# A third raw weight buffer in the gates' own pool, and the weight sums' work buffer from the trunk on

## The chip, the cores and the metric

The kernel runs on one core of a Trainium2 chip. The metric is device time in microseconds (us) from the start to the end of one execution. Its engines are TensorE (PE, with PEld for its weight loads), VectorE (DVE), ScalarE (ACT), GpSimd (POOL) and SyncE (SP). SP computes nothing here: it issues most of the DMAs, one after the other in the order of its queue, and a DMA that has to wait holds those behind it in the queue. POOL issues some DMAs as well.

## The reference

One layer of a streaming encoder for two groups of tokens that share the weights: 1024 prompt frames and 32 sample frames, width 1024, all in f32.

```python
z = rms_norm(x, g_mix) @ w_in
q, k, v, ch, cb, cc, ga, gb = split(z)
a  = window_attention(q, k, v, sink) @ w_attn_out
bo = (cb * causal_conv3(cc * ch)) @ w_conv_out
x  = x + (sigmoid(ga) * a + sigmoid(gb) * bo) @ w_mix_out
x  = x + memory_attention(rms_norm(x, g_cross) @ w_cq, mem_k, mem_v) @ w_co
x  = x + square(relu(rms_norm(x, g_mlp) @ w_up)) @ w_down
y  = rms_norm(x, g_final)
```

The keys and values of the window, the convolution's state and the memory's keys and values are returned beside y.

## The kernel before, in words

The 1056 tokens lie on the free axis in three chunks (384, 384, 288) and the features on the 128 partitions. A weight is a tile of 128 x 1024 f32 (512 KB). For f32 accuracy every operand is split in two: `split` casts the raw tile to `wh` (ACT, L129) and subtracts that to get `wl` (DVE, L130), and a product is three matmuls (`gemm`, L193 to L195; `product` for half a weight, L864 to L866).

Weights come in the order of the list `worder`. `fetch_w` (L147) issues the load of the next raw tile on SP (L155) and puts it on the list `fetched`; `issue_w` takes the first of that list, or fetches if there is none, and splits it into `wh` and `wl` (three buffers each); `next_w` keeps three split weights ready. Raw tiles have two buffers, tag `wr`. From the gates on there is a third: when the dictionary `third` is not empty, it counts the fetches, and every third one takes the tile `ws` of the pool `W["pool"]`, which has one buffer.

That tile is also the work buffer of the weight sums. The gates, and parts of the MLP, use products of a Strassen kind, which need sums of weight quarters. `sum_step` makes them piece by piece on POOL: it issues the load of a piece (L712, L714) into one of two tiles (`ws` and `xacc`, in turn), adds four times in the tile loaded by the step before (L719), and issues that tile's store (L723, L725) to `gsum_d` (gates), `wsum_d` (w_down) or `usum_d` (w_up). There are 50 pieces: 14 for the gates, 32 for w_down, 4 for w_up, in this order. The steps are called among the other work from the fourth attention host to the end of the attention output; in the order of the program all are done before the gates. The trace gives the two tiles the names `ws` and `xacc` by their buffers.

The stages around the change are, in the order of the program:
- the hosts: 32 weights of w_in (convolution inputs marked C, H and B, queries, keys), with window attention between their chunks; `do_KS` loads the key cache `ck` of a group of heads (L518, one buffer);
- the attention output: eight weights for three chunks (`do_attn_out`), with the last sum steps between;
- the gates: seven pairs, `gate_pair(f)` for f = 1 to 7. A pair uses four weights, w1 = w_in 34+f, w4 and w3 (the two sums of pair f), and w2 = w_in 42+f. It loads the attention's output (`load_a`, L928), stores the gated one (`attended`, L920), and `pump` loads and splits operands (L794, L795, L799). It begins, for f = 1, with `third["n"] = 2` and a fetch: that of w3, which so takes the third buffer;
- the trunk: conv_out, mix and the memory attention for each chunk, and then the MLP (up, down), where the sums of w_up and w_down are read.

The order in each engine's queue is made before the run by the framework's planner. It runs through a plan of its own, with its own estimates of durations, and puts an instruction in its engine's queue when, in the plan, its inputs and its buffer are there. The order of the program decides between instructions that are ready together. `pin` (`keep_in_program_order`) puts an instruction behind the one traced before it on its engine; the sum steps are pinned on POOL, the loads of weights on SP are not. Pools with `reuse_waits="tile"` may be opened on memory of closed pools: a new tile waits for the old tiles that lay there.

Memory: the pool `gtop` of the gates (`Y["top"]`) holds, per partition, eight tiles N4 and one each of s1, u2 and v, of 1536 bytes, 16,896 in all. It is opened where `ytop` (16 x 1152 = 18,432 bytes, operands of the attention output's third chunk) was.

```python
        if third and third["n"] % 3 == 0:
            raw = W["pool"].tile([P, 4, 256], F32, tag="ws", name=nm("wr3")).rearrange("p q c -> p (q c)")
        else:
            raw = wp.tile([P, 1024], F32, tag="wr", bufs=2, name=nm("wr"))
        src = weight(worder[wpos[0] + len(fetched)])
        sp.dma_start(raw.rearrange("p (i c) -> p i c", i=4) if len(src.shape) == 3 else raw, src)
```

Of the kernel before, what the change touches and what calls it, by code (L numbers as in the profile page):

```python
# [10 lines left out]
F32 = mybir.dt.float32  # L11
# [7 lines left out]
P = 128  # L19
# [4 lines left out]
NF = 8  # L24
# [16 lines left out]
def hybrid_step(ctx: ExitStack, tc: tile.TileContext, io):  # L41
# [5 lines left out]
    def nm(s):  # L47
        uid[0] += 1
        return f"{s}_{uid[0]}"

    def opened(name, **kw):
        cm = tc.tile_pool(name=name, **kw)
        return cm, cm.__enter__()

    def closed(cm):
        cm.__exit__(None, None, None)
# [43 lines left out]
    def acc_tile(shape):  # L100
        return ps.tile(shape, F32, tag="acc", bufs=n_acc, name=nm("acc"))
# [3 lines left out]
    def tmp(n, dt=F32):  # L105
        return tp.tile([P, n], dt, tag="ct", bufs=NCT, name=nm("ct"))
# [25 lines left out]
    def weight(key):  # L132
        name, *at = key
        if name in ("w_down", "w_sum"):
            q, j, t = at
            return (wsum_d if name == "w_sum" else io[name])[j, t, :, :, q].rearrange("i p c -> p i c")
        if name == "g_sum":
            return gsum_d[at[0]][:, at[1]].rearrange("p h c -> p (h c)")
        src = io[name]
        for j in at:  # L140
            src = src[j]
        return src

    fetched = []
    third = {}

    def fetch_w():  # L147
        if third:
            third["n"] += 1
        if third and third["n"] % 3 == 0:  # L150
            raw = W["pool"].tile([P, 4, 256], F32, tag="ws", name=nm("wr3")).rearrange("p q c -> p (q c)")
        else:
            raw = wp.tile([P, 1024], F32, tag="wr", bufs=2, name=nm("wr"))
        src = weight(worder[wpos[0] + len(fetched)])
        sp.dma_start(raw.rearrange("p (i c) -> p i c", i=4) if len(src.shape) == 3 else raw, src)  # L155
        fetched.append(raw)

    def issue_w():
        if not fetched:
            fetch_w()  # L160
        raw = fetched.pop(0)
        key = worder[wpos[0]]
        hi = wp.tile([P, 1024], F32R, tag="wh", name=nm("wh"))
        lo = wp.tile([P, 1024], F32R, tag="wl", name=nm("wl"))
        if kept.get(key) is not None:
            sp.dma_start(lo.bitcast(F32), kept[key])
            act.copy(hi, raw)
        else:
            split(hi, lo, raw)
            if key in kept:  # L170
                kept[key] = dram.tile([P, 1024], F32, name=nm("wl_d"))
                sp.dma_start(kept[key], lo.bitcast(F32))
        ready.append((worder[wpos[0]], (hi, lo)))
        wpos[0] += 1
# [39 lines left out]
    def xacc_tile():  # L214
        xacc[0] = tp.tile([P, 1056], F32, tag="xacc", name=nm("xacc"))
        return xacc[0]
# [59 lines left out]
    W = {}  # L276
# [11 lines left out]
    def norm_x():  # L288
# [7 lines left out]
        def load_x():  # L296
            for c, (o, n) in enumerate(CH):
                raw = raw_tile()[:, : NF * n].rearrange("p (f t) -> p f t", f=NF)
                for h in range(4):
                    sp.dma_start(raw[:, 2 * h : 2 * h + 2], io[f"x{c}"][:, 2 * h : 2 * h + 2])  # L300
                    if c == h == 0:
                        sp.dma_start(prm, io["params"])
                        fetch_w()
                if c == 0:
                    fetch_w()
                    fetch_w()
                raws.append(raw)
# [345 lines left out]
    def gate_slot(c, f):  # L653
        n = CH[c][1]
        return slot(ga_pool, f"Ga{c}", n, F32) if f < 3 else slot(G["pool"], f"Gb{c}", n, F32)
# [36 lines left out]
    pieces = [("g", f, q) for f in PAIRS for q in range(2)]  # L692
# [42 lines left out]
    for i, h in enumerate(hosts):  # L735
        kv, p = i // 8, i % 8
# [26 lines left out]
    Y = {}  # L763
# [27 lines left out]
    def pump(n):  # L791
        for into, at, t, get in coming:
            hi, lo = into[at] = (get(), get())
            pin(act.copy(hi, t))  # L794
            pin(dve.tensor_sub(lo, t, hi.bitcast(F32)))  # L795
        coming.clear()
        for into, at, src, cols, get in wanted[:n]:
            t = cols() if callable(cols) else tmp(cols)
            sp.dma_start(t, src)  # L799
            coming.append((into, at, t, get))  # L800
        del wanted[:n]
# [57 lines left out]
    def product(acc, w, half, acts, start):  # L859

        wh, wl = w
        for k, (hi, lo) in enumerate(acts):
            a = slice(512 * half + k * P, 512 * half + k * P + P)
            pe.matmul(acc, wh[:, a], hi, start=(start and k == 0), stop=False, skip_group_check=True)  # L864
            pe.matmul(acc, wh[:, a], lo, start=False, stop=False, skip_group_check=True)  # L865
            pe.matmul(acc, wl[:, a], hi, start=False, stop=(k == 3), skip_group_check=True)  # L866
# [22 lines left out]
    def gate_c2(w):  # L889
        n = CH[2][1]  # L890
        a = ps.tile([P, n], F32, tag="pt", bufs=2, name=nm("pa"))
        gemm(a, w, xg[2])
        return a
# [14 lines left out]
    def gate_pair(f):  # L908
        def take(key):
            k, w = ready.pop(0)  # L910
            assert k == key, (k, key)
            return w

        def into(t, x):
            act.activation(t, x, AF.Sigmoid)
            return t

        def attended(c, t):
            dve.tensor_mul(t, t, la[c])
            sp.dma_start(m1_d[c][:, f], t)  # L920

        la = {}

        def load_a(c):
            if (c, f) in sa:
                return
            la[c] = tmp(CH[c][1])
            sp.dma_start(la[c], a_d[c][:, f])  # L928

        op = lambda kind: [gop[kind, k] for k in range(4)]  # L930
        w1 = take(("w_in", 34 + f))
        if f == 1:
            assert not pieces and "new" not in W
            third["n"] = 2
            fetch_w()
        load_a(0)
        load_a(2)
        A, B, C = (acc_tile([P, 384]) for _ in range(3))
        product(A, w1, 0, op("b11"), True)
        s1 = Y["top"].tile([P, 384], F32, tag="s1", name=nm("s1"))  # L940
        act.copy(s1, A)
        issue_w()
        if f < NF - 1:
            fetch_w()
        product(A, w1, 1, op("b21"), False)
        attended(0, into(tmp(384), A))
        pump(4 if f == 1 else 1)
        if (2, f) not in sa:
            a2 = gate_c2(w1)
            t = tmp(CH[2][1])  # L950
            dve.tensor_mul(t, a2, R[2])
            attended(2, into(t, t))
        issue_w()
        fetch_w()
        w4 = take(("g_sum", f - 1, 0))
        product(B, w4, 0, op("t2"), True)
        load_a(1)
        u2 = Y["top"].tile([P, 384], F32, tag="u2", name=nm("u2"))
        dve.tensor_sub(u2, B, s1)
        sum_step()  # L960
        pump(4 if f == 1 else 1)
        w3 = take(("g_sum", f - 1, 1))
        product(C, w3, 1, op("n1"), True)
        v = Y["top"].tile([P, 384], F32, tag="v", name=nm("v"))
        dve.tensor_add(v, C, s1)
        product(B, w3, 0, op("n3"), False)
        g22 = gate_slot(1, f)
        dve.tensor_sub(g22, B, v)
        sg[1][f] = into(g22, g22)
        pump(0)  # L970
        sum_step()
        product(C, w4, 1, op("b22"), False)
        t = tmp(384)
        dve.tensor_sub(t, C, u2)
        attended(1, into(t, t))
        issue_w()
        fetch_w()
        w2 = take(("w_in", 42 + f))
        product(B, w2, 1, op("n4"), False)
        g21 = gate_slot(0, f)  # L980
        dve.tensor_sub(g21, B, s1)
        sg[0][f] = into(g21, g21)
        sum_step()
        issue_w()
        fetch_w()
        a2 = gate_c2(w2)
        g2 = gate_slot(2, f)
        dve.tensor_mul(g2, a2, R[2])
        sg[2][f] = into(g2, g2)
# [18 lines left out]
    for f in PAIRS:  # L1008
        worder.extend([("w_in", 34 + f), ("g_sum", f - 1, 0), ("g_sum", f - 1, 1), ("w_in", 42 + f)])
        item(lambda f=f: gate_pair(f))  # L1010
# [6 lines left out]
    def after_gates():  # L1017
        nonlocal m_cm, mpool, cr_cm, cr
        assert not pieces and "new" not in W
        closed(x_cm)  # L1020
        xacc_tile()
        m_cm, mpool = opened("mpool", bufs=18, reuse_waits="tile")
        cr_cm, cr = opened("cross", bufs=1, reuse_waits="tile", side="right")

    item(after_gates)


# [243 lines left out]
    top = {}  # L1271
# [711 lines left out]
```

## Time and profile before

| | us |
|---|---|
| median of 3 runs | 1853.06 (1849.84 to 1855.01) |
| the profiled execution | 1852.53 |
| its span | 1850.8 |
| PE busy | 1727.6 (93%) |
| DVE busy | 1180.8 (64%) |
| ACT busy | 853.8 (46%) |
| POOL busy | 567.9 (31%) |
| mean DMA rate | 189 GB/s |

The mean granted clock of TensorE is 0.971 of full speed. In the profile's page the span is cut in 40 equal slices; a digit is the busy share of a slice in tenths. A row of waits names who waited, for whom, the total in us, how often, and the longest. A row of a timeline gives start and duration in us, engine, line, operation, what is written and from what, how many instructions are merged, and in brackets the idle time before and what ended it. A row of windows gives a stretch, its length, then each engine's busy time with its instructions, the clock, the DMA share and GB/s. A row of DMA issues gives what is loaded or stored, the queue, how many, the size, and the median time in us from issue to landing. A row of groups gives line, operation and shapes, count, busy time, the mean of one in ns, and the idle time before.

### The profile page before, as it was taken

Reading aid. Unit: us, or ns where it says so; the run is one execution under the profiler, and the core shown is the slowest. Engines: PE = TensorE matmul, PEld = TensorE weight load, DVE = VectorE, ACT = ScalarE, POOL = GpSimd, SP = SyncE. Lnnn points to the kernel's source line nnn. Section 1 sums busy time; section 2 is a strip of 40 time slices with the busy share of each in tenths; the row PEclk is TensorE's granted clock in tenths of the full one; section 3 lists DMA queues with packets and bytes.
Section 4 is the critical chain, followed back from the end, with each engine's and each line's share of the span. In section 5 each row is a group of like instructions: output and inputs, shape, how many; then the busy total and the mean of one; then the engine's idle time right before and its main releaser. Section 6 shows DMA issues by size and latency. Waiting matters only on the chain.

```text
span 1850.8 us, 32562 instructions
## 1 busy us (share of the span) xinstructions
PE 1727.6 (93%) x12250; PEld 1713.2 (93%) x12250; DVE 1180.8 (64%) x2270; ACT 853.8 (46%) x1660; POOL 567.9 (31%) x651
## 2 busy tenths in 40 slices
PE   8999999999999940699999999999999999999998
PEld 8999999999999940699999998999999999999998
DVE  7776767767667610444656777868766677546575
ACT  8644535344344210333445565566444454333353
POOL 0026464643544445200122513001555620100121
PEclk9999999999999975799999999999999999999999
DMA  5323343434348863454876566765766686555554
GB/s 181 116 95 135 109 144 128 158 128 139 134 152 306 284 221 125 140 184 139 270 262 207 195 215 226 254 223 199 238 227 223 220 288 229 181 191 168 191 173 162
DMA packets 182221, 349.75 MB, mean 189 GB/s; under 512 B 19744, under 2 KB 102976, under 8 KB 181936
## 3 DMA queue, kind: packets, MB, share of 16 engines
q1 hardware_dynamic: 167008, 295.07, 47.1%
q0 software_dynamic: 15056, 52.60, 7.9%
q8 instruction: 96, 1.57, 0.3%
q14 instruction: 61, 0.50, 0.1%
HBM read 252.82 MB, written 94.19 MB: 187 GB/s over the span
## 4 chain that ended last, share of the span: by engine, by line
PE 81%; DMA 8%; POOL 5%; DVE 2%; issue 2%; ACT 1%; SPq 0%; DVEq 0%; ACTq 0%; POOLq 0%
PE acc L193 10%; PE acc L195 10%; PE acc L194 10%; PE acc L1768 6%; PE acc L1770 6%; PE acc L1769 6%; PE acc L864 6%; PE acc L866 6%; PE acc L865 6%; DMA wsum_d<-xacc 2%; DMA wsum_d<-ws 2%; POOL ws L719 2%; POOL xacc L719 2%; PE pc L865 2%; PE pc L866 2%
## 5 line engine op out<-in xcount | busy, mean ns | idle before, releaser
L129 ACT CAST wh<-wr 128x1024 fp32r<-128x1024 f32 x226 | 237.3, 1050 | 502.4 <-PE acc L1769 123.8
L130 DVE TENSOR_TENSOR wl<-wr,wh 128x1024 fp32r<-128x1024 f32 x226 | 292.2, 1293 | 200.6 <-ACT wh L129 198.9
L193 PE MATMUL acc<-X,wh 128*128 128x384 f32 (+1 forms) x864 | 282.1, 327 | 7.7 <-ACT wh L129 7.7
L194 PE MATMUL acc<-X,wh 128*128 128x384 f32 (+1 forms) x864 | 279.2, 323 | 0.0
L195 PE MATMUL acc<-X,wl 128*128 128x384 f32 (+1 forms) x864 | 278.6, 323 | 0.2 <-DVE wl L130 0.2
L269 POOL TENSOR_TENSOR xacc<-xacc,ct 128x384 f32<-128x384 f32 (+1 forms) x56 | 75.5, 1352 | 400.6 <-ACT ct L267 399.0
L193 PEld LDWEIGHTS acc<-X,wh 128*128 128x128 f32 x864 | 163.1, 189 | 8.3 <-ACT wh L129 7.7
L194 PEld LDWEIGHTS acc<-X,wh 128*128 128x128 f32 x864 | 163.4, 189 | 0.6
L195 PEld LDWEIGHTS acc<-X,wl 128*128 128x128 f32 x864 | 163.0, 189 | 0.8 <-DVE wl L130 0.8
L195 PE MATMUL acc<-Y,wl 128*128 128x384 f32 (+1 forms) x432 | 139.8, 324 | 2.1 <-DMA wl<-wl_d 2.1
L194 PE MATMUL acc<-Y,wh 128*128 128x384 f32 (+1 forms) x432 | 139.8, 324 | 0.0
L193 PE MATMUL acc<-Y,wh 128*128 128x384 f32 (+1 forms) x432 | 139.4, 325 | 0.3 <-ACT Y L774 0.3
L864 PE MATMUL acc<-X,wh 128*128 128x384 f32 x112 | 38.3, 343 | 91.4 <-ACT wh L129 91.4
L864 PEld LDWEIGHTS acc<-X,wh 128*128 128x128 f32 x112 | 21.5, 192 | 91.7 <-ACT wh L129 91.7
L1769 PE MATMUL acc<-n,wh 128*128 128x264 f32 x352 | 100.2, 285 | 0.0
L1768 PE MATMUL acc<-n,wh 128*128 128x264 f32 x352 | 100.2, 285 | 0.0
L1770 PE MATMUL acc<-n,wl 128*128 128x264 f32 x352 | 100.0, 285 | 0.0
L129 ACT CAST PTh<-pt 128x512 fp32r<-128x512 f32 (+3 forms) x94 | 45.9, 517 | 112.4 <-PE pt L582 111.7
L1049 POOL TENSOR_TENSOR ct<-ct,ct 128x384 f32<-128x384 f32 (+1 forms) x21 | 23.1, 1100 | 233.4 <-DMA wr<-in_w_conv_out 142.6
L719 POOL TENSOR_TENSOR ws<-ws 128x256 f32<-128x256 f32 x100 | 86.0, 860 | 5.6
L719 POOL TENSOR_TENSOR xacc<-xacc 128x256 f32<-128x256 f32 x100 | 83.8, 838 | 5.5 <-DMA xacc<-in_w_in 0.2
L195 PEld LDWEIGHTS acc<-Y,wl 128*128 128x128 f32 x432 | 81.6, 189 | 2.4 <-DMA wl<-wl_d 2.4
(422 smaller groups left out, 5643.4 us busy)
## 6 DMA issues: line engine op xcount, KB each, us to landing
wr<-in_w_in SPq DMA_DIRECT2D x53, 512.0 KB, 3.7
wr<-in_w_up SPq DMA_DIRECT2D x53, 512.0 KB, 4.3
wr<-wsum_d SPq DMA_DIRECT2D x40, 512.0 KB, 3.4
wr<-in_w_conv_out SPq DMA_DIRECT2D x24, 512.0 KB, 4.1
wr<-in_w_mix SPq DMA_DIRECT2D x24, 512.0 KB, 5.4
wr<-in_w_down SPq DMA_DIRECT2D x24, 512.0 KB, 3.6
wl<-wl_d SPq DMA_DIRECT2D x18, 512.0 KB, 4.8
n_d<-Z SPq DMA_DIRECT2D x32, 264.0 KB, 4.1
```

Of the source, the lines that this page charges most:

```text
L129: act.copy(hi, src)
L130: dve.tensor_sub(lo, src, hi.bitcast(F32))
L193: pe.matmul(out, wh[:, a], hi, start=(k == 0), stop=False)
L194: pe.matmul(out, wh[:, a], lo, start=False, stop=False)
L195: pe.matmul(out, wl[:, a], hi, start=False, stop=(k == len(acts) - 1))
L719: pin(pool_e.tensor_tensor(t[:, to], t[:, x], t[:, y], op=ALU.add))
L864: pe.matmul(acc, wh[:, a], hi, start=(start and k == 0), stop=False, skip_group_check=True)
L865: pe.matmul(acc, wh[:, a], lo, start=False, stop=False, skip_group_check=True)
L866: pe.matmul(acc, wl[:, a], hi, start=False, stop=(k == 3), skip_group_check=True)
L1768: pe.matmul(a, wh[:, s], hi, start=(t == 0 and k == 0), stop=False, skip_group_check=True)
L1769: pe.matmul(a, wh[:, s], lo, start=False, stop=False, skip_group_check=True)
L1770: pe.matmul(a, wl[:, s], hi, start=False, stop=(t == 1 and k == 7), skip_group_check=True)
```

## The change

The third buffer's pool becomes an entry of `third`. In the gates, from f = 1, it is a tile `ws` of the gates' own pool `gtop`, 4096 bytes more a partition. At the beginning of the last pair (f = 7) `third` is emptied, so that the fetches of that pair (its w2, conv_out 0 to 2) go to the two `wr` buffers. Behind the gates, in `after_gates`, `third` is filled again with the count at 0 and the sums' pool `W["pool"]`: the third fetch from there (conv_out 5) takes the work buffer `ws`. The assertion that all sum pieces are done at f = 1 goes; the sum steps are called where they were.

```diff
@@ fetch_w
         if third and third["n"] % 3 == 0:
-            raw = W["pool"].tile([P, 4, 256], F32, tag="ws", name=nm("wr3")).rearrange("p q c -> p (q c)")
+            raw = third["pool"].tile([P, 4, 256], F32, tag="ws", name=nm("wr3")).rearrange("p q c -> p (q c)")
         else:
@@ gate_pair
         if f == 1:
-            assert not pieces and "new" not in W
-            third["n"] = 2
+            third.update(n=2, pool=Y["top"])
             fetch_w()
+        if f == NF - 1:
+            third.clear()
@@ after_gates
         closed(x_cm)
         xacc_tile()
+        third.update(n=0, pool=W["pool"])
```

## The prediction

> **What bounds the kernel now.** I read the page's engine slices first, then the waits between 660 and 770 us, then the queues of PE, SP and POOL in order of time. TensorE is busy 93% of the span, and the share is lost in one place:
>
> ```profile
> span 1850.8 us, 32562 instructions
> PE   8999999999999940699999999999999999999998
> PEclk9999999999999975799999999999999999999999
> ```
>
> Slices 14 to 16 (46.3 us each) hold nearly all of PE's idle time. The waits there, then SP's own:
>
> ```profile
> PE acc L864 <- ACT wh L129: 91.4, 1, 91.4
> ACT wh L129 <- DMA wr<-gsum_d: 88.1, 1, 88.1
> ...
> SPq L155 <- DMA ws<-in_w_up: 73.0, 2, 72.3
> ```
>
> PE waits 91.4 us once, for a split that waits for a load that SP does not issue. The orders of PE and SP show where:
>
> ```profile
> 657.39 0.34 PE L864 MATMUL acc<-X,wh 128*128 128x384 f32 x1
> ...
> 666.55 0.33 PE L865 MATMUL acc<-X,wh 128*128 128x384 f32 x1
> 666.73 0.34 PE L866 MATMUL acc<-X,wl 128*128 128x384 f32 x1
> 758.42 0.69 PE L864 MATMUL acc<-X,wh 128*128 128x384 f32 x1 [91.36 <-ACT wh L129]
> ...
> 889.50 0.34 PE L193 MATMUL acc<-Y,wh 128*128 128x384 f32 x1
> ...
> 655.34 0.42 SPq L928 DMA_DIRECT2D ct<-a_d  x1
> ...
> 669.33 1.52 SPq L799 DMA_DIRECT2D ct<-bc_d  x3
> 753.77 7.34 SPq L155 DMA_DIRECT2D wr<-gsum_d  x3
> ```
>
> This is the first gate pair (f = 1): w1's products (from 657.39) and w4's first are done, and the product with the operand n1 needs `w3`, the sum (g_sum, 0, 1). Its raw load is the first to go to the third buffer, which today is the weight sums' work buffer `ws`. The data in DRAM were written long before; the buffer is what is late. So the stage is bound by the end of the sums, which POOL works through alone, one piece a step: load, four adds, store, and the next load waits for that store.
>
> ```profile
> 555.97 0.56 POOL L725 DMA_DIRECT2D wsum_d<-xacc  x1 [0.41 <-POOL xacc L719]
> ...
> 670.92 0.57 POOL L725 DMA_DIRECT2D wsum_d<-ws  x1 [0.41 <-POOL ws L719]
> ...
> 680.23 0.57 POOL L725 DMA_DIRECT2D wsum_d<-xacc  x1 [0.41 <-POOL xacc L719]
> ...
> 709.88 0.57 POOL L725 DMA_DIRECT2D wsum_d<-xacc  x1 [0.41 <-POOL xacc L719]
> ...
> 718.25 0.57 POOL L725 DMA_DIRECT2D wsum_d<-ws  x1 [0.41 <-POOL ws L719]
> ...
> 749.98 1.45 POOL L723 DMA_DIRECT2D usum_d<-ws  x2 [0.41 <-POOL ws L719]
> ```
>
> Beside the attention output (555.97 to 670.92, 11 steps) a step takes 10.45 us; alone (680.23 to 709.88, 4 steps) 7.41. After the 18th `wsum` store at 718.25 the four `usum` pieces take 31.7 us more, and the last lands 3.8 us after its start, at 753.77.
>
> **The change, part by part.**
>
> *The first raw load (gain 91.4 us, less 2).* The buffer moves into the gates' own pool. That pool opens on the memory of `ytop`, whose tiles are read last by the attention output's last chunk, which ends where w1's matmuls begin, at 657.4; so the load can go then at the earliest.
>
> ```profile
> wr<-gsum_d SPq DMA_DIRECT2D x1, 512.0 KB, 4.2
> ...
> wr<-in_w_in SPq DMA_DIRECT2D x3, 512.0 KB, 6.0
> ...
> L129 ACT CAST wh<-wr 128x1024 fp32r<-128x1024 f32 x226 | 237.3, 1050 | 502.4 <-PE acc L1769 123.8
> L130 DVE TENSOR_TENSOR wl<-wr,wh 128x1024 fp32r<-128x1024 f32 x226 | 292.2, 1293 | 200.6 <-ACT wh L129 198.9
> ...
> 666.20 2.98 ACT L794 CAST Y<-Gb 128x384 fp32r<-128x384 f32 x7
> ```
>
> Landing takes 4.2 to 6.0 us beside the attention output, the cast 1.05: ready at 663 to 665, before PE asks at 667.1; the wait would be 0. The other bound is a cast queued behind the activation splits that ACT runs until 669.2 (2.1 after PE asks, plus its own 1.05): 3.2. I take 2, nearer the upper bound, because SP also has loads and stores of this pair to issue then. A wait of 2 us should leave the clock alone:
>
> ```profile
> 670.00:680.00 10.00, 0.00 (x0) 0.00 (x0) 2.80 (x5) 0.00 (x0) 4.51 (x7) 0.57 0.62 221
> ```
>
> A mean of 0.57 over ten microseconds, in a page row that falls from full to 5 tenths, says that the clock fell some 1.4 us into them, 4 after PE's last matmul.
>
> *The work buffer from the trunk on (cost 23 us).* Here I differ from the change's wording. In the last pair the third buffer is dropped, and `n` starts at 0 behind the gates; the third trunk fetch (conv_out weight 5) takes `ws`. That is after the gates in program order, but not in SP's queue. The planner puts a load into the queue as soon as its buffer is free in the plan. The key cache of the second attention group shows it:
>
> ```profile
> 96.55 0.33 SPq L518 DMA_DIRECT2D ck<-in_cache_k  x1
> ...
> 192.93 0.30 ACT L129 CAST ckh<-ck 128x128 fp32r<-128x128 f32 x1
> ```
>
> That load was queued 96 us ahead of its use, right when its one buffer came free. So the trunk's `ws` load will stand in SP's queue where the plan thinks that the sums end, and SP will halt there until they really end. Both times have to be estimated.
>
> When does the plan end the sums? POOL's queue tells, in the hosts' stage:
>
> ```profile
> 387.64 0.59 POOL L725 DMA_DIRECT2D wsum_d<-xacc  x1 [0.42 <-POOL xacc L719]
> ...
> 396.06 0.57 POOL L725 DMA_DIRECT2D wsum_d<-ws  x1 [0.28 <-POOL S L559]
> 399.06 0.18 POOL L644 COPY cvt<-u 128x2 f32<-128x2 f32 x1 [2.43 <-DVE u L626]
> 399.41 0.53 POOL L714 DMA_DIRECT2D ws<-in_w_down  x1 [0.16 <-issue]
> 399.94 0.79 POOL L645 COPY cvt<-u 128x2 f32<-128x2 f32 x1
> ```
>
> L644 and L645 wait for two successive DVE products behind the same PE chunk, and the sum's next load L714, which waits for the store, was queued between them. In the plan, then, the store landed between them too: measured against PE, the plan's step there is the chip's, 396.06 - 387.64 = 8.4, less 0.2 for a copy in it, 8.2. I let it vary by 0.6. If the plan holds 8.2 through the attention output, where the chip needs 10.45, then it has the 18th store at 555.97 + 17 x 8.2 = 695.4; the `usum` pieces at 31.7 plus 3 x 0.8 (8.2 less 7.41) take it to 729.5 and a landing 0.7 longer than 3.8 to 734. With the 2 us above, SP gets there at 736, gates under way for 76 of their 138 us (657.4 to 667.1 and 758.4 to 889, less 2.5 for the slow clock; an estimate from PE's rows).
>
> When do the sums end? They now run beside the gates.
>
> ```profile
> 551.00:657.00 106.00, 105.71 (x675) 105.39 (x674) 67.43 (x94) 38.23 (x73) 48.62 (x61) 1.00 0.84 295
> ...
> 767.00:875.00 108.00, 108.00 (x670) 108.00 (x669) 54.91 (x80) 41.96 (x66) 0.00 (x0) 1.00 0.51 169
> ```
>
> Gates alone move 169 GB/s; the sums' two 512 KB a step add 100, together 269 against 295 beside the attention output. So a step is nearer 10.45 than 7.41: I take 9.8. From 670.92, six steps and 0.9 for the first `w_up` load give 730.6, the `usum` pieces 31.7 plus two longer steps of 2.4 give 767, landing 770 (bounds 754 and 777).
>
> SP is then held from 736 to 770. PE lives on what is fetched:
>
> ```profile
> 828.13 0.33 SPq L155 DMA_DIRECT2D wr<-gsum_d  x1
> ...
> 843.81 1.05 ACT L129 CAST wh<-wr 128x1024 fp32r<-128x1024 f32 x1 [0.60 <-PE acc L865]
> ```
>
> Counted by fours (four fetches, four casts a pair), this is the same weight: 15.7 us. PE stops at about 752 and starts again at 770 plus 4.65 (753.77 to 758.42 today), 774.7: idle 23.
>
> Whether the gates slow the sums rests on what a store takes:
>
> ```profile
> wsum_d<-xacc POOLq DMA_DIRECT2D x5, 512.0 KB, 5.7
> ...
> wsum_d<-xacc POOLq DMA_DIRECT2D x3, 512.0 KB, 2.9
> ```
>
> 5.7 us beside the attention output (551 to 660), 2.9 alone (680 to 720). With the shorter landing throughout, the sums would keep today's end, 754, PE would be idle for 754 + 4.65 - 752 = 6.6, and the sum would be 1771, a rival below. That is what a page of the Trainium skill, "DMA: Bandwidth & Descriptors", section "Anatomy of one DMA — SWDGE (gpsimd) path", comes to: it gives a transfer from GpSimd 2.0 us plus its bytes by 436 GB/s, an estimate of 3.2 for 512 KB, with no term for what runs beside it. The stage with traffic does not agree, 5.7.
>
> *Two buffers for six fetches (cost 1 us).* The last pair's own weight and conv_out 0 to 4 share two raw buffers. A buffer's turn is 6.0 plus 1.05 plus 1.29, 8.3, so 4.2 a weight, against 24 matmuls 0.18 apart (666.55, 666.73), 4.3. It just hides, under the weights fetched before; bounds 0, and 3 if each load waits 1 us in SP's queue (six by 0.5). I take 1.
>
> *Everything else* has one answer: the same adds, stores, casts and matmuls are issued, and the sums are read only in the MLP, at the end of the kernel.
>
> **Sum.** The profiled execution took 1852.53 (span 1850.8), 0.5 below the median of 1853.06. 91.4 - 2 - 23 - 1 = 65.4; 1852.5 - 65.4 = 1787.
>
> **The rivals.**
> - *SP never stops: the plan's sums end no earlier than the chip's* (a plan that slows its DMAs as the chip does, a step of 9.8 or more for 8.2; each 0.1 is worth 2.1 us by the 21 steps' worth above). Then 91.4 - 2 - 1: 1764. Against it the tie at 399 us; for it, that the tie comes from a stage with less traffic.
> - *The gates do not slow the sums* (a step of 7.41): 1771, as above. Against it the landings of 5.7.
> - *SP stops much sooner*: a plan step of 6.1 puts the load at 692, and PE stops at 708. Of the six steps 3.8 are done by then, 2.2 run alone (16.3), and with 0.9, 31.7 and 3.8 the sums end at 761; PE restarts at 765.7 after 57.7 idle: gain 91.4 - 2 - 57.7 - 1 = 31, 1822. The plan's end cannot lie before 670.85, since today's waiting load was queued behind the three bc loads.
> - *The change does not free the load*: if the new buffer's memory is released late, PE still waits to 758: 1853, no change. The pool grows by 4 KB past `ytop`, but what lay there belonged to the attention, closed before the attention output.
> - *Slower*: the trunk's `ws` load stands ahead of the whole first pair. Then the 12 issues of 655.34 to 670.85, done today during the wait, come after 753.8: 12 x 0.4 plus a landing of 4 is 9 us more, 1862. It decides if the plan ends the sums before 655, a plan step of under 4.5 us; the tie speaks against that.
>
> **How the numbers follow.** My forecast 0.44, own range 1771 to 1806 (plan step 7.6 to 8.8 is 13 us either way, sums' step 9 to 10.45 some 6, the two small terms 4). No stop 0.23 (1761 to 1771). Sums not slowed 0.07. Sooner stop 0.16 (1806 to 1848). No change 0.04; slower 0.06, other shifts of the plan behind the gates included. A change under 0.3% (5.6 us) could not be told from none. Faster 0.90, within 0.04, slower 0.06. Range 1761 to 1822: it leaves out the upper part of the sooner stop (0.08) and the last two.
>
> **What would show it.** PE's wait before `w3` is 0 to 4 us. SP's waits name `ws<-in_w_up` or `usum_d` once, of 20 to 45 us, with a conv_out load behind it in the midst of the gates, and PE's idle time there is some 16 us less. `wsum_d` stores beside the gates come 9 to 10.5 us apart. PE's slices show one digit of 4 to 6 about slice 16 in place of 4, 0 and 6. I am wrong if no conv_out load stands among the gate fetches (then 1764), or if the plan's step in the attention output is not that of the hosts.

## The result and the profile after

The changed kernel takes 1776.8 us (median of 4 runs, 1775.5 to 1778.1), the kernel before 1852.5 (median of 4 runs, 1849.8 to 1855.0). The ratio of the times is 0.9592, 95% interval 0.9575 to 0.9608. A second group of runs gave 1780.1 (median of 4) and a ratio of 0.960 (0.9585 to 0.9615). The prediction was faster, 1787 us.

The head of the page of the changed kernel, with PE's busy slices and the granted clock:

```profile
span 1776.3 us, 32569 instructions
...
PE   8999999999999999979999999999999999999998
...
PEclk9999999999999999989999998999999999999999
```

The profiled execution took 1778.09 us, 1.3 above the median. The hole of 4, 0 and 6 tenths about slice 16 is gone; one digit of 7 is left at slice 17 (755 to 799 us; the first slice counts as 0, as in the prediction). Its waits, PE's between 655 and 830 us:

```profile
PE acc L864 <- ACT wh L129: 10.0, 2, 9.4
PE acc L864 <- DVE Ga L982: 0.9, 1, 0.9
```

and the two of SP's own between 640 and 830 us that name the work buffer:

```profile
SPq L155 <- DMA ws<-in_w_up: 16.3, 2, 15.4
SPq L155 <- DMA usum_d<-ws: 9.8, 1, 9.8
```

PE's one wait of 91.4 us has become one of 9.4, for the same thing as before, a split. SP still stops for the work buffer `ws`, 15.4 + 9.8 = 25.2 us in its two long waits. What stands in SP's queue there (the loads of line L155 in SP's order of time):

```profile
656.52 0.32 SPq L155 DMA_DIRECT2D wr<-gsum_d  x1
...
752.34 0.33 SPq L155 DMA_DIRECT2D wr<-in_w_in  x1
778.99 0.33 SPq L155 DMA_DIRECT2D wr<-in_w_conv_out  x1
779.42 0.38 SPq L155 DMA_DIRECT2D wr<-in_w_in  x1
```

The load at 656.52 is `w3` of the first pair. It goes out as PE begins w1's products (656.46) and waits for nothing in its new buffer. The one at 778.99 is conv_out weight 5: behind the gates in the program, but between two gate weights in the queue, held from 752.7 to 779.0. The casts of ACT (line L129), that of `w3` first, then the last before the gap and the first behind it, tell what PE had left to live on:

```profile
661.66 1.05 ACT L129 CAST wh<-wr 128x1024 fp32r<-128x1024 f32 x1 [2.41 <-DMA wr<-gsum_d]
...
762.71 1.05 ACT L129 CAST wh<-wr 128x1024 fp32r<-128x1024 f32 x1 [4.72 <-PE acc L865]
784.61 1.04 ACT L129 CAST wh<-wr 128x1024 fp32r<-128x1024 f32 x1 [20.12 <-DMA wr<-in_w_in]
```

and PE's own order shows the first product of `w3`, the first wait in the gates, and the restart:

```profile
665.97 0.33 PE L864 MATMUL acc<-X,wh 128*128 128x384 f32 x1
...
676.26 0.45 PE L864 MATMUL acc<-X,wh 128*128 128x384 f32 x1 [0.65 <-ACT wh L129]
...
785.70 0.69 PE L864 MATMUL acc<-X,wh 128*128 128x384 f32 x1 [9.38 <-ACT wh L129]
```

The operands' names alone don't tell the weights apart; the order of the program and of the casts does. From 661.77 to 667.88 PE makes 36 products without a pause, twelve each of w1, w4 and, from 665.97, `w3`. So `w3` is ready in time. The wait of 0.65 at 676.26 is for w1 of the second pair, whose cast began at 675.16.

In windows (length, PE busy, granted clock, DMA share, GB/s) the changed kernel's gates and what follows them are

```profile
657.40:752.70 95.30, 93.29 (x570) 92.04 (x569) 60.50 (x80) 40.95 (x69) 45.00 (x53) 1.00 0.80 271
752.70:776.30 23.60, 23.60 (x148) 23.31 (x146) 9.03 (x13) 5.14 (x9) 17.16 (x22) 1.00 0.33 112
776.30:785.70 9.40, 0.03 (x1) 0.00 (x0) 0.02 (x1) 1.09 (x2) 0.19 (x1) 0.60 0.76 253
785.70:809.90 24.20, 24.20 (x133) 24.08 (x134) 13.10 (x19) 9.49 (x15) 0.00 (x0) 0.87 0.55 183
...
905.90:1193.90 288.00, 278.68 (x1953) 0.97 0.65 219
...
809.90:1776.30 966.40, 943.07 (x7161) 0.99 0.64 216
```

(the first four with all engines, PE first; the last two with PE alone, the second of them to the end of the span), and the same stretches behind the gates of the kernel before, whose gates end at 889.1:

```profile
985.10:1273.10 288.00, 274.69 (x1964) 0.99 0.64 220
...
889.10:1850.80 961.70, 938.07 (x7161) 0.99 0.64 216
```

The balance by PE, with the end of the gates taken as the end of their last product with an operand N: from 657.4 to there it was 231.7 us (889.1), now 152.5 (809.9), a gain of 79.2; 0.9 of it is that the gates begin at 656.46 and not at 657.39. PE's idle time there is 2.0 in the first window and 9.4 in the third, where it was 91.4. From the gates' end to the end of the span it was 961.7, now 966.4, a loss of 4.7. So the span gains 79.2 - 4.7 = 74.5. The loss is not idle time: PE idles 23.6 us there before and 23.3 after, but the same 7161 matmuls are busy for 938.07 and 943.07, 5.0 more. The granted clock says where: over the 288 us that begin 96 us behind the gates it is 0.99 before and 0.97 after, 2% of 288 or some 6 us, as far as two digits tell. The last section shows the stretches at half clock that make up the difference.

The loss is no accident of one execution. The kernel of the first experiment below waits as the kernel before does and takes 962.2 us behind the gates, PE busy for 937.3; the changed kernel, profiled once more, takes 967.0 and 942.7.

### The profile page after: what moved, and what is told of

It reads as the page before. It is cut to its first block, busy times and chain, and to the rows that moved or that the text cites. A ratio compares the mean times of both kernels' runs of the same rounds, so it can differ in the third digit from the quotient of the medians.

```text
span 1776.3 us, 32569 instructions
## 1 busy us (share of the span) xinstructions
PE 1734.2 (98%) x12250; PEld 1716.3 (97%) x12250; DVE 1184.4 (67%) x2270; ACT 852.8 (48%) x1660; POOL 576.8 (32%) x651
## 4 chain that ended last, share of the span: by engine, by line
PE 77%; DMA 11%; POOL 6%; DVE 2%; issue 2%; ACT 2%; SPq 0%; DVEq 0%; POOLq 0%; ACTq 0%
PE acc L193 10%; PE acc L195 10%; PE acc L194 10%; PE acc L1772 6%; PE acc L1770 6%; PE acc L1771 6%; PE acc L864 5%; PE acc L866 5%; PE acc L865 5%; DMA wsum_d<-ws 3%; DMA wsum_d<-xacc 3%; POOL ws L719 2%; POOL xacc L719 2%; PE pc L864 2%; PE pc L865 2%
## 5 line engine op out<-in xcount | busy, mean ns | idle before, releaser
L129 ACT CAST wh<-wr 128x1024 fp32r<-128x1024 f32 x226 | 237.2, 1050 | 424.5 <-PE acc L1771 126.2
L193 PEld LDWEIGHTS acc<-X,wh 128*128 128x128 f32 x864 | 163.0, 189 | 7.2 <-ACT wh L129 6.6
L194 PEld LDWEIGHTS acc<-X,wh 128*128 128x128 f32 x864 | 163.1, 189 | 0.7
L1770 PE MATMUL acc<-n,wh 128*128 128x264 f32 x352 | 100.2, 285 | 0.0
L1771 PE MATMUL acc<-n,wh 128*128 128x264 f32 x352 | 100.1, 284 | 0.0
L129 ACT CAST PTh<-pt 128x512 fp32r<-128x512 f32 (+3 forms) x94 | 46.0, 516 | 111.6 <-PE pt L582 110.8
L719 POOL TENSOR_TENSOR ws<-ws 128x256 f32<-128x256 f32 x100 | 91.9, 919 | 5.6
L719 POOL TENSOR_TENSOR xacc<-xacc 128x256 f32<-128x256 f32 x100 | 87.9, 879 | 5.5 <-DMA xacc<-in_w_in 0.2
L193 PEld LDWEIGHTS acc<-Y,wh 128*128 128x128 f32 x432 | 80.9, 188 | 0.7 <-ACT Y L774 0.7
L194 PEld LDWEIGHTS acc<-Y,wh 128*128 128x128 f32 x432 | 81.1, 188 | 0.0
L864 PE MATMUL acc<-n,wh 128*128 128x264 f32 x256 | 72.9, 285 | 0.8 <-DVE Z L1502 0.8
```

The source lines that it names most:

```text
L129: act.copy(hi, src)
L193: pe.matmul(out, wh[:, a], hi, start=(k == 0), stop=False)
L194: pe.matmul(out, wh[:, a], lo, start=False, stop=False)
L719: pin(pool_e.tensor_tensor(t[:, to], t[:, x], t[:, y], op=ALU.add))
L1770: pe.matmul(a, wh[:, s], hi, start=(t == 0 and k == 0), stop=False, skip_group_check=True)
L1771: pe.matmul(a, wh[:, s], lo, start=False, stop=False, skip_group_check=True)
```

## The experiments

All edits are made in the changed kernel. The times are medians, the ratios are to the kernel before, run beside them. Where gates are said to end, it is the end of their last product with an operand N.

*Is it the gates' own buffer that brings the gain?* The last part of the change is kept, the first put back:

```diff
-            third.update(n=2, pool=Y["top"])
+            third.update(n=2, pool=W["pool"])
```

> The change with one part put back: the gates' third raw buffer is the sums' work buffer again; the drop of the third buffer in the last pair and the new count behind the gates stay. Theory (the whole gain is the gates' own buffer): PE waits some 91 us again in the first pair, for the split of the weight that waits for the sums, and the time is 1848 to 1858; the load behind the gates costs nothing, since the sums are over before it. Rival (a good part of the gain comes from the trunk's count, or from another order of the plan): under 1840.

1854.9 us, ratio 1.000 (0.9985 to 1.0015). PE's waits and SP's, in this order:

```profile
PE acc L864 <- ACT wh L129: 93.1, 1, 93.1
```

```profile
SPq L155 <- DMA ws<-in_w_up: 74.0, 2, 73.2
```

The wait is back at its old size, and the trunk's part of the change costs nothing where the sums are over by then. The theory holds: the whole gain hangs on the gates' own buffer, and the trunk's load into `ws` stops nothing when the sums are over before it.

*Do the gates need a third buffer at all?* Here `third` stays empty until the trunk:

```diff
         if f == 1:
-            third.update(n=2, pool=Y["top"])
             fetch_w()
```

> The changed kernel without a third raw buffer in the gates: the pairs have the two wr buffers, the trunk's use of the work buffer is as in the changed kernel. Theory (what counted was that no gate load waits for the work buffer; a pair's four loads in 18 us fit two buffers of 8.3 us a turn): PE's waits in the gates grow by 0 to 5 us, 1775 to 1783. Rival (the third buffer itself is worth much in the gates, because loads take 5 to 6 us beside the sums): 1785 or more, with PE waits for wh in every pair.

1782.7 us, ratio 0.9631 (0.9606 to 0.9656); the gates end at 810.3, as in the changed kernel (809.9). SP stops here too, from 755.9 until conv_out goes out at 769.46, and PE has one long wait in the gates:

```profile
PE pa L193 <- ACT wh L129: 6.4, 1, 6.4
```

The stop is shorter than in the changed kernel, mostly because the sums end sooner: their last store is issued at 766.3 instead of 775.8. Why they end sooner wasn't tried. Nearly all of the gain is had with two buffers: what counted was to take `w3` off the work buffer, not to have a third one. What a third one is worth to the gates, 6 us at most between 1776.8 and 1782.7, isn't settled by intervals that just touch (0.9575 to 0.9608 and 0.9606 to 0.9656). The profiled execution is the fastest of the four (1776.7; the others took 1782.1 to 1787.8), so the wait of 6.4 needn't be that of the median.

*Does the place of SP's stop follow from the plan, and not from the place in the program?* The count behind the gates begins at -6 and takes no third buffer at 0 or below, so that the ninth trunk fetch, not the third, is the first to take `ws`:

```diff
-        if third and third["n"] % 3 == 0:
+        if third and third["n"] > 0 and third["n"] % 3 == 0:
...
-        third.update(n=0, pool=W["pool"])
+        third.update(n=-6, pool=W["pool"])
```

> The changed kernel, but the first fetch that takes the work buffer behind the gates is the ninth, not the third (a mix weight, needed some 25 us later). Theory (the place in SP's queue is the point at which the plan frees the buffer, whatever the load is for): the stop stays where it was, at 752 +- 3, as long as it was, 25 +- 3 us, now with the mix weight behind it, and PE waits 9 +- 2 us; time 1777 +- 3. Rival (the place follows the order of the program, a few weights ahead of the use): the stop moves behind the end of the sums and vanishes, about 1767.

1777.5 us, ratio 0.9594 (0.955 to 0.9637). The two runs are 11 us apart (1771.8 and 1783.2), so the time says little here and the trace decides. SP's loads of line L155 in order of time:

```profile
755.97 0.33 SPq L155 DMA_DIRECT2D wr<-in_w_in  x1
782.58 0.33 SPq L155 DMA_DIRECT2D wr<-in_w_mix  x1
```

Another load, six weights later in the program (a mix weight), stands between the same two gate weights and stops SP as long: from 756.3 to 782.6, 26.3 us as in the changed kernel, with a PE wait of 9.2. It begins 3.6 us later than there, a little outside the 3 allowed; the first pair's `w3` load is late by 2.1 (658.60) already. The rival fell: in this kernel's plan the load into `ws` is queued where the plan frees the buffer, whichever load it is and however far ahead of its use.

*What is the stop worth?* The trunk's first load into `ws` is put behind the load traced before it on SP:

```diff
-        sp.dma_start(raw.rearrange("p (i c) -> p i c", i=4) if len(src.shape) == 3 else raw, src)
-        fetched.append(raw)
+        load = sp.dma_start(raw.rearrange("p (i c) -> p i c", i=4) if len(src.shape) == 3 else raw, src)
+        fetched.append(pin(load) and raw if third.get("n") == 3 and third["pool"] is W["pool"] else raw)
```

> The changed kernel, but the first load into the work buffer behind the gates (conv_out 5) is pinned on SP behind the load traced before it, so that it can't stand among the gates' loads. Theory (the load's place in SP's queue costs the remaining wait): SP's stop of 25 us (752.3 to 779.0) is gone, PE's wait of 9.4 us in the gates too, gates end near 800 instead of 809.6; time 1776.8 - 9.4 = 1767 (1764 to 1770). Rival (PE's wait in the sixth pair has another cause, the loads being slowed by the sums beside them): the wait stays, 1775 to 1779.

1770.1 us, ratio 0.9555 (0.9533 to 0.9578), at the upper edge of what was expected. Neither `ws` nor `usum_d` is among SP's waits, PE's wait of 9.4 is gone, the gates end at 800.7, 9.2 earlier. So the stop costs what was said, as far as the gates go. But not all of it arrives, and the intervals of the two times just overlap. Behind the gates this kernel takes 972.0 us, 5.6 more than the changed one. The first 48.2 us of the trunk, of this kernel

```profile
800.70:848.90 48.20, 44.79 (x251) 1.00 0.87 292
```

and of the changed one

```profile
809.90:858.10 48.20, 48.20 (x279) 1.00 0.85 295
```

show 3.4 us of new idle time, at the place where six fetches share two buffers. That the two buffers are its cause is argued, not shown. The stop had hidden it: in the changed kernel four trunk loads are out before the gates end (778.99 to 807.02), one of them the held one, in the pinned kernel three (779.59 to 797.78).

*Is the trunk's third buffer worth its stop?* It is left out:

```diff
-        third.update(n=0, pool=W["pool"])
```

> The changed kernel without a third raw buffer behind the gates: the trunk has the two wr buffers alone. Theory: the wait of 9.4 us in the gates is gone as with the pinned load, and the trunk pays little for the missing buffer (the prediction put six such fetches at 1 us): 1766 to 1773. Rival (the third buffer carries the trunk): 1780 or more, with new PE waits for wh behind 800.

1773.7 us, ratio 0.9574 (0.9554 to 0.9594), just above the expected range. No stop of SP, gates done at 799.0, but 975.7 us from there to the end (966.4 in the changed kernel), with one long wait in the trunk (the next one is 2.7)

```profile
PE acc L193 <- ACT wh L129: 6.5, 1, 6.5
```

So the third trunk buffer is worth about what its stop costs; the intervals of this kernel, of the changed one and of the pinned one overlap.

*Both costs taken away.* The gates' third buffer serves through the last pair, the count runs on behind the gates, and the first load into `ws` is held in order:

```diff
-        sp.dma_start(raw.rearrange("p (i c) -> p i c", i=4) if len(src.shape) == 3 else raw, src)
+        load = sp.dma_start(raw.rearrange("p (i c) -> p i c", i=4) if len(src.shape) == 3 else raw, src)
+        if third.get("n") == 33:
+            pin(load)
...
-        if f == NF - 1:
-            third.clear()
...
+        if f == NF - 1:
+            third["pool"] = None
...
-        third.update(n=0, pool=W["pool"])
+        third["pool"] = W["pool"]
```

> The change with both later costs taken away at once: the gates' third buffer serves on through the last pair and the fetches for the trunk made in it, so that no six fetches share two buffers; behind the gates the count runs on in the sums' work buffer, and the first load into it is held in SP's queue behind the load that stands before it in the program. Theory (the stop of SP costs the 9.4 us of PE before the gates' restart, and the two buffers cost the 3.4 us at the start of the trunk that show once the stop is gone): no SP wait that names the work buffer, no PE wait over 2 us in the gates, PE busy at least 47 of the trunk's first 48 us, and 1766 (1763 to 1770). Rival (what is lost behind the gates is the plan's other order of the memory attention and does not depend on buffers): the gates end by 801 and the time is still 1770 to 1777.

1766.2 us (5 runs, 1764.3 to 1766.7), ratio 0.9523 (0.9508 to 0.9538). The changed kernel ran beside it:

> The changed kernel once more, beside the others on one chip. Both theories: 1775 to 1779, with SP's stop between 752 and 779 us.

1780.1 us, ratio 0.960 (0.9585 to 0.9615), a little above the range expected, with the stop in its place. The version with both costs taken away is so the fastest, 13.9 us below the changed kernel on the same chip, with intervals far apart. The two profiles are 13.3 apart: 10.9 because the gates end sooner (799.0 for 809.9), and 2.4 behind them. Its page, and in windows the first 48.2 us of its trunk and the whole stretch from there to the end:

```profile
span 1763.6 us, 32574 instructions
...
PE   8999999999999999999999999999999999999998
...
PEclk9999999999999999999999999999999999999999
```

```profile
798.90:847.10 48.20, 46.65 (x264) 1.00 0.86 281
...
798.90:1763.60 964.70, 940.68 (x7161) 0.99 0.65 216
```

No slice is left with a hole, no wait of SP names `ws` or `usum_d`, and PE's longest wait in the gates is 1.0. PE is busy for 46.65 of the trunk's first 48.2 us (47 was expected) and loses 1.5, less than the 3.4 of the pinned kernel. Behind the gates it takes 964.7 us, 3.0 above the kernel before, and 2.6 of that is again PE's busy time, not its waits. What in this version lessens that loss isn't shown, and the step from the pinned kernel to this one (0.9555 to 0.9523) lies within overlapping intervals.

## Why the prediction was right, step by step

The likeliest case of the prediction is what happened, mechanism by mechanism; the time is 10 us under the forecast, inside its own range. The stop of SP cost 13.6 less than forecast and two buffers 1 less; against that stand 4.7 lost behind the gates, at which the sum put nothing, and 0.8 within them (91.4 - 2.0 - 9.4 is 80.0, and 79.2 was gained there). So the span gained 74.5 where the sum says 65.4. That it came so near is in part luck: within the stop three terms were off by 8 to 17 us each and partly cancelled.

*The first raw load (91.4, less 2).* Right. `w3`'s product has no wait at all where 2 us were taken; the lower bound, 0, was met. The load went out at 656.52, with w1's first product, as the prediction had it. PE's idle time up to the stop is 2.0 all the same, in short waits elsewhere (0.65 for the next w1, 0.94 for DVE): that the 2 came out is luck.

*The stop of SP (cost 23).* The mechanism is right to the weight: conv_out 5 in SP's queue amid the gates, held until the last `usum` store has landed, PE fed from what was fetched. The cost is 9.4 and not 23, because three of the step's terms were mis-sized:
- Where the plan has the sums end: SP gets there at 752.7 instead of 736. By the prediction's own rule (2.1 us for each 0.1 of the plan's step) this is a plan step of 8.2 + 0.8 = 9.0 instead of the 8.2 read from the hosts. That is outside the 7.6 to 8.8 that the prediction allowed, and it had named such a difference between the attention output and the hosts as a sign of being wrong. The plan can't be seen itself, so the 9.0 is inferred.
- When the sums end: 779.0 instead of 770. Step and `usum` pieces were both longer:

```profile
669.25 0.57 POOL L725 DMA_DIRECT2D wsum_d<-ws  x1 [0.41 <-POOL ws L719]
...
734.17 0.57 POOL L725 DMA_DIRECT2D wsum_d<-ws  x1 [0.41 <-POOL ws L719]
...
775.05 1.45 POOL L723 DMA_DIRECT2D usum_d<-ws  x2 [0.41 <-POOL ws L719]
```

  Six steps between the first two rows, 64.9 us, are 10.8 each; 9.8 was taken, and 10.45 was the upper bound. From the last `wsum` store to the last `usum` store it is 40.9 us, where 31.7 plus 4.8 was taken.
- How long PE lives on: 15.7 was taken, from a load's issue to the cast of the same weight. PE stopped at 776.3, 24.0 after the last load (752.34). That load was cast at 762.71, in the last cast before the gap, 10.4 after its issue, and PE ran for 13.6 us more on the split weights that stood ready. The step ended at the cast where it should have ended at the last product.

PE restarts at 785.7, 6.7 after SP goes on, where 4.65 was taken: the held load goes out first, the gate weight behind it at 779.42, and its cast begins 5.2 later (3.6 in the kernel before, 753.77 to 757.33). The sum of the errors: PE's stop 24.3 later (776.3 for 752), its restart 11.0 later (785.7 for 774.7), so 13.3 less idle time, 9.4 for 22.7.

*Two buffers for six fetches (cost 1).* Nothing in the changed kernel, since the stop covers it: PE is busy through all of the trunk's first 48.2 us. In the pinned kernel, without that cover, 3.4 in that stretch, a little above the upper bound of 3.

*"Everything else has one answer."* This is what the prediction lacked: 4.7 us lost behind the gates. The same matmuls are issued, as it says, but not in the same order (last section), and shifts of the plan behind the gates had a share in one chance and no price. PE's idle time there did not grow; its busy time grew by 5.0 at a lower granted clock.

*The rivals.* SP doesn't stop: refuted by the waits, and built, it is the pinned kernel, 1770 for the 1764 named. The gates don't slow the sums: refuted, and by two kernels that run the same adds; the adds of the sums (line L719) in the changed kernel, from 660 to 780 us,

```profile
L719 POOL TENSOR_TENSOR ws<-ws 128x256 f32<-128x256 f32 x24 | 24.6, 1026 | 1.5
```

and with the gates halted, in the kernel whose gates wait for `ws` (671 to 754 us):

```profile
L719 POOL TENSOR_TENSOR ws<-ws 128x256 f32<-128x256 f32 x20 | 14.5, 725 | 1.3
```

An add in `ws` takes 1026 ns beside the gates and 725 alone (917 and 725 in `xacc`). A store's landing grows as well; the sums' stores in the changed kernel, from 657 to 735 us:

```profile
wsum_d<-xacc POOLq DMA_DIRECT2D x4, 512.0 KB, 5.6
wsum_d<-ws POOLq DMA_DIRECT2D x4, 512.0 KB, 4.2
```

against 2.9 alone. The estimate of 3.2 us by the Trainium skill ("DMA: Bandwidth & Descriptors", section "Anatomy of one DMA — SWDGE (gpsimd) path") is near the store alone and not beside traffic.

The stop that comes much sooner, no change, and slower didn't happen. Of the signs named, the wait at `w3` (0) and SP's stop with conv_out behind it are as said. The stores were to be 9 to 10.5 us apart and are 10.8 in the mean (8.1 to 12.9). PE's idle time is 17 less than SP's stop of 26.3 where 16 was said, but the digit in PE's slices is 7 instead of 4 to 6, and one slice further on.

## What to carry to other kernels

When a buffer is shared with a slow side job, look for the load that waits for it and for what stands behind that load in its queue: moving the buffer turned a wait of 91 us into one of 9, and the load that took the buffer next stopped the queue for 26 us, long ahead of its own use. A load whose buffer is freed by another engine's long chain is best held in program order on its queue (here the gates end 9 us sooner by it and the kernel some 7, by intervals that just overlap, since it lays bare another cost). When costing how long an engine survives a stopped queue, count from the last load that got out to the last product made with it, not to its cast.

## What the runs showed of the hardware that was not expected

PE can lose time without waiting longer: the same 7161 matmuls took 5.0 us more behind the gates while idle time was unchanged, at a granted clock of 0.97 for 0.99 over 288 us. Narrow windows in those 288 us find the stretches at half clock, first in the changed kernel, then in the kernel before:

```profile
1064.99:1068.40 3.41, 3.41 (x16) 0.50 0.59 198
1095.71:1102.53 6.82, 6.01 (x27) 0.50 0.78 282
1150.32:1153.73 3.41, 3.41 (x16) 0.50 0.93 278
1163.97:1167.38 3.41, 3.41 (x17) 0.50 1.02 402
```

```profile
1176.64:1180.05 3.41, 3.09 (x14) 0.50 0.68 226
1234.67:1238.08 3.41, 3.41 (x18) 0.50 1.06 378
```

They are 17.1 us against 6.8. Half of the difference, 5.1 us, is an estimate of what they cost, and fits the 5.0. The second profiles of both behaviours have the same two sums, 17.1 (the changed kernel once more) and 6.8 (the gates' buffer put back into `ws`). The longest waits of PE from 1000 to 1195 us are

```profile
PE acc L864 <- ACT lt L1324: 2.3, 1, 2.3
PE acc L193 <- DVE Ga L1065: 1.9, 1, 1.9
```

So the clock fell in a stage with no wait over 2.3 us. The prediction's reading that a wait of 2 us leaves the clock alone wasn't tested in the gates, where the longest wait before the stop is 0.9 and the clock 1.00. Here it does not hold: the second stretch at half clock, from 1095.71, begins inside the wait of 2.3 us, which ends at 1096.52. The Trainium skill ("TensorE: Matmul & The Clock Gate", section "HAM oscillation — how this bites in real kernels") asks for no idle gap above some 3.4 us; by that rule alone it should have stayed full, and the rows disagree. What lowered it more after the change than before stays open. A candidate that wasn't tried: the plan puts part of the memory attention in another order. By the names of their operands PE's matmuls come in one order behind the gates in both profiles with 6.8 us at half clock and in another in both with 17.1, and the two orders differ from the 1383rd to the 2795th of the matmuls.

POOL's adds and DVE's operations on two SBUF inputs are slower beside each other. DVE's products of line L919 in the gates, in the changed kernel from 660 to 752 us with the sums beside them, and in the kernel before from 780 to 880 without:

```profile
L919 DVE TENSOR_TENSOR ct<-ct,ct 128x384 f32<-128x384 f32 x9 | 8.0, 892 | 0.0
```

```profile
L919 DVE TENSOR_TENSOR ct<-ct,ct 128x384 f32<-128x384 f32 x11 | 6.1, 551 | 0.0
```

892 against 551 ns, while an add on POOL goes from 725 to 1026. DVE's operations with one input from PSUM (`acc`, the accumulator that PE writes) are not slower in the same two windows, with the sums and without:

```profile
L960 DVE TENSOR_TENSOR u<-acc,s 128x384 f32<-128x384 f32 x5 | 2.8, 550 | 2.3 <-issue 1.3 <-PE acc L866 1.0
```

```profile
L959 DVE TENSOR_TENSOR u<-acc,s 128x384 f32<-128x384 f32 x5 | 2.8, 553 | 4.1 <-PE acc L866 4.1
```

So it isn't the heavier traffic as such that slows DVE. The Trainium skill ("SBUF — State Buffer", section "SBUF: two separate sides") says that an operation of VectorE with two SBUF inputs and one of GpSimd that reads SBUF hold a shared pair of ports in turn; these rows agree with it. PE hardly notices here: of its waits from 655 to 830 us 1.1 us name DVE. How much of the longer landings comes from the other transfers (271 GB/s in the window from 657.4) and how much from DVE wasn't tried apart.
